# One hybrid decoder layer on eight cores: three phases in a row, or projections and output layer placed between attention tasks

## The chip, the cores and the metric

The kernel runs on all eight cores of one Trainium2 chip, two cores for each of the four batch entries. The metric is the device time of the slowest core in microseconds (us). Six runs of the kernel before had a median of 803.76 us. Some runs of any kernel on all cores fall into a slower state of the chip (one of these six did, with 835.79 us). Engines: PE is the matmul array, PEld its weight loads, DVE the vector engine, ACT the activation engine, POOL the GpSimd engine, SP the engine that issues plain transfers.

## The reference

```python
z = h @ w_in                                  # (B, 4096, 3072): q, k, v, gate, u, pool gate
s = einsum('bqhcd,bkhcd->bhcqk', q, k) / 8    # 4 heads, two halves c of width 64
a = softmax(where(causal, s, -inf))           # per half
o = (a[:, :, 0] - lam * a[:, :, 1]) @ v       # differential attention
o = rms_norm(o, subln_g) * (1 - lam_init) * silu(g_attn)
y = (trailing_mean_over(2, 4, 8, 16)(u) - u) @ w_pool * scale * silu(g_pool)
h = layer_norm(ALPHA * x + concat(o, y) @ w_out, ln_g, ln_b)
h = h + (p @ w_pe) * sigmoid(h @ w_pg + b_pg)
```

Width is 1024, sequence 4096, four heads. Each core makes keys and values for the whole sequence of its batch entry, and everything else for its half of the queries.

## The kernel before

The program has an in-order list of work for each engine, and a helper adds the semaphore waits from what each operation reads and writes. It runs in three phases. First come all projections, over eight accumulator banks in turn:

```python
for kc in range(8):                                   # one chunk: 8 matmuls of 512 columns
    matmul(ps[:, bank, :], win[:, kc, fc*128:(fc+1)*128], xbuf[:, kc, :], ...)
evac_copy(bank, kT[:, h, s*GT:(s+1)*GT], ...)         # DVE and ACT in turn
```

Then comes attention, one key block of 128 against 512 queries at a time:

```python
matmul(ps[:, 2*sl+c, q0:512], kT[64*c:64*c+64, h, keys], qT[64*c:64*c+64, h, queries])   # QK, c = 0, 1
activation(PT[pi], ps[:, 2*sl:2*sl+2], Exp)                                              # ACT, 1,024 wide
tensor_tensor(Lacc, Lacc, PT[pi], add)                # DVE: row sums; every second or third step
                                                      # goes to PE instead, as ones_bf @ PT
matmul(ps[:, 4+c, q0:512], Vt[keys, head], PT[pi][:, c, q0:512])                         # AV, V stationary
...
```

At the end comes the output layer, one tile of 128 tokens after another: `w_out`, layer norm, transpose, `w_pg`, sigmoid, `w_pe`.

The softmax here doesn't subtract the row's maximum and nothing guards it: scores larger than these inputs give would overflow.

## Time and profile before

| | before |
|---|---|
| median of six runs | 803.76 us |
| profiled run, slowest core | 805.6 us, mean granted clock 0.978 |
| busy: PE, DVE, ACT | 719.5, 562.3, 437.5 us |
| projections / attention / output layer | to 260 / to 643 / to the end |

A busy PE is not one at its peak, because matmuls overlap and their ends are modelled. The clock column is the share of full array clock that was granted.

### The profile page before, as it was taken

How to read it: one execution, taken by the hardware profiler on the slowest of the kernel's cores; microseconds unless marked ns; L12 is line 12 of the kernel's file. 1: busy time of each engine (PE TensorE's matmuls, PEld its weight loads, DVE VectorE, ACT ScalarE, POOL GpSimd, SP SyncE). 2: the span in 40 equal slices, each digit the busy share in tenths (PEclk: the TensorE clock that was granted, in tenths of full speed). 3: DMA queues.
4: the chain of work that ended last, by engine and by line, in shares of the span. 5: the costliest groups of instructions: out<-in, count | busy, mean ns of one | idle time of the engine just before them, and what ended most of it. 6: DMA issues, size and time to landing. Idle time of an engine off the chain costs nothing.

```text
span 805.6 us, 8871 instructions; the slowest of 8 cores (795.8 to 805.6 us)
## 1 busy us (share of the span) xinstructions
PE 719.5 (89%) x3496; PEld 278.6 (35%) x3496; DVE 562.3 (70%) x665; ACT 437.5 (54%) x526; POOL 87.3 (11%) x76
## 2 busy tenths in 40 slices
PE   0798999999999978888889889989898989999994
PEld 0343444444443322222222222222222335445441
DVE  0121723624535678888899989989889988888883
ACT  0012112112122889999989898999899932222221
POOL 6000000000000100000000000000000024544551
PEclk9999999999999999999999999999999999999997
DMA  8998330330300980000000000000003013343321
GB/s 89 141 158 112 53 52 1 53 53 0 53 1 0 137 152 0 1 1 1 0 1 1 0 1 1 0 1 1 1 0 131 1 52 105 106 147 115 105 105 52
DMA packets 28106, 39.96 MB, mean 50 GB/s; under 512 B 7328, under 2 KB 21024, under 8 KB 28064
## 3 DMA queue, kind: packets, MB, share of 16 engines
q0 software_dynamic: 22160, 20.81, 18.8%
q1 hardware_dynamic: 5904, 18.59, 7.3%
q8 instruction: 27, 0.44, 0.2%
q14 instruction: 15, 0.12, 0.0%
HBM read 51.81 MB, written 8.39 MB: 75 GB/s over the span
## 4 chain that ended last, share of the span: by engine, by line
PE 65%; DVE 14%; ACT 14%; DMA 3%; issue 2%; POOL 1%; another core or an unknown queue 0%; DVEq 0%; ACTq 0%; POOLq 0%
PE psum_all L332 20%; PE psum_all L545 9%; ACT sb_PT L520 8%; DVE sb_Lacc L531 7%; PE psum_all L372 7%; PE psum_all L727 6%; PE psum_all L667 6%; PE psum_all L505 6%; DMA sb_win<-w_in 3%; PE psum_all L550 3%; PE psum_all L714 2%; ACT sb_PT L516 2%; ACT sb_rr L571 2%; PE psum_all L702 2%; ACT sb_rr L575 1%
## 5 line engine op out<-in xcount | busy, mean ns | idle before, releaser
L531 DVE TENSOR_TENSOR sb_Lacc<-sb_Lacc,sb_PT 128x1024 f32<-128x1024 f32 (+1 forms) x200 | 232.0, 1160 | 28.3 <-ACT sb_PT L520 18.0
L520 ACT ACTIVATE sb_PT<-psum_all 128x1024 bf16<-128x1024 f32 (+3 forms) x256 | 228.9, 949 | 27.7 <-PE psum_all L505 16.4
L332 PE MATMUL psum_all<-sb_xb,sb_win 128*128 128x512 bf16 x768 | 170.2, 384 | 20.8 <-DMA sb_win<-w_in 20.8
L545 PE MATMUL psum_all<-sb_PT,sb_Vt 128*128 128x512 bf16 (+3 forms) x640 | 185.7, 373 | 0.6
L505 PE MATMUL psum_all<-sb_qT,sb_kT 64*128 64x512 bf16 (+3 forms) x640 | 120.9, 375 | 22.2 <-ACT sb_PT L520 18.3
L332 PEld LDWEIGHTS psum_all<-sb_xb,sb_win 128*128 128x128 bf16 x768 | 75.6, 99 | 113.3 <-issue 25.0
L505 PEld LDWEIGHTS psum_all<-sb_qT,sb_kT 64*128 64x128 bf16 x640 | 30.6, 93 | 159.8 <-ACT sb_PT L520 90.3
L516 ACT ACTIVATE sb_PT<-psum_all,sb_maskb 128x1024 bf16<-128x1024 f32 x64 | 67.8, 1110 | 6.0 <-PE psum_all L505 3.6
L686 POOL TENSOR_SCALAR sb_mv<-sb_mv 128x1 f32<-128x1 f32 x16 | 21.0, 1311 | 399.6 <-DVE sb_mv L679 399.6
L372 PE MATMUL psum_all<-sb_win,sb_xb 128*128 128x512 bf16 x256 | 58.3, 387 | 4.2 <-DMA sb_win<-w_in 4.2
L545 PEld LDWEIGHTS psum_all<-sb_PT,sb_Vt 128*128 128x128 bf16 x640 | 40.5, 98 | 59.9 <-issue 53.9
L667 PE MATMUL psum_all<-sb_wout,sb_mixT 128*128 128x512 bf16 x256 | 57.9, 379 | 0.5 <-DVE sb_Vt L672 0.5
L550 PE MATMUL psum_all<-sb_PT,sb_ones_bf 128*128 128x512 bf16 (+2 forms) x208 | 58.1, 362 | 0.0
L727 PE MATMUL psum_all<-sb_wpg,sb_kT 128*128 128x512 bf16 x256 | 57.9, 379 | 0.0
L737 ACT ACTIVATE sb_Vt<-sb_Vt 128x1024 f32<-128x1024 f32 x16 | 16.9, 1057 | 73.8 <-DVE sb_Vt L733 73.8
L744 POOL TENSOR_TENSOR sb_qT<-sb_qT,sb_Vt 128x1024 f32<-128x1024 f32 x15 | 35.4, 2359 | 59.5 <-DVE sb_qT L740 59.5
L318 DVE CAST sb_Vt<-psum_all 128x512 bf16<-128x512 f32 x16 | 11.1, 692 | 43.2 <-PE psum_all L372 43.2
L323 ACT ACTIVATE sb_Vt<-psum_all 128x512 bf16<-128x512 f32 x16 | 9.6, 597 | 55.3 <-PE psum_all L372 55.3
L318 DVE CAST sb_kT<-psum_all 128x512 bf16<-128x512 f32 x16 | 11.1, 691 | 40.1 <-PE psum_all L332 40.1
L396 ACT ACTIVATE sb_gps<-psum_all 128x512 f32<-128x512 f32 x16 | 9.6, 597 | 52.3 <-PE psum_all L332 52.3
L372 PEld LDWEIGHTS psum_all<-sb_win,sb_xb 128*128 128x128 bf16 x256 | 25.4, 100 | 35.9 <-DMA sb_win<-w_in 4.7
L708 ACT ACTIVATE sb_kT<-psum_all 128x512 bf16<-128x512 f32 x32 | 17.4, 595 | 34.1 <-PE psum_all L702 34.1
(96 smaller groups left out, 664.8 us busy)
## 6 DMA issues: line engine op xcount, KB each, us to landing
sb_xb<-xT POOLq DMA_DIRECT2D x8, 1024.0 KB, 10.2
sb_kT<-x_own SPq DMA_DIRECT2D x16, 512.0 KB, 4.9
out<-sb_qT SPq DMA_DIRECT2D x16, 512.0 KB, 3.6
sb_win<-w_in POOLq DMA_DIRECT2D x5, 1024.0 KB, 46.3
sb_wout<-w_out POOLq DMA_DIRECT2D x1, 2048.0 KB, 18.4
sb_wpg<-w_pg POOLq DMA_DIRECT2D x1, 2048.0 KB, 31.1
sb_win<-w_in POOLq DMA_DIRECT2D x4, 256.0 KB, 19.9
sb_pTb<-pT POOLq DMA_DIRECT2D x1, 1024.0 KB, 34.7
```

Source lines behind the costliest of these rows:

```text
L318: P.op(DVE, lambda e: e.tensor_copy(out=out_ap, in_=src), reads=[B_bank[bank]], writes=wbufs)
L332: P.op(PE, lambda e, kc=kc: e.matmul(ps[:, bank, :], win[:, kc, fc * 128:(fc + 1) * 128], xbuf[:, kc, :], start=(kc == 0), stop=(kc == 7)) ...
L372: st_=(kc == 0), sp_=(kc == 7): e.matmul(o, a, b, start=st_, stop=sp_),
L505: P.op(PE, lambda e, c=c: e.matmul(ps[:, 2 * sl + c, q0:512], kT[64 * c:64 * c + 64, h, key0:key0 + 128], qT[64 * c:64 * c + 64, h, j * GT ...
L516: P.op(ACT, lambda e: e.activation(out=PT[pi][:, :, q0:512], in_=ps[:, 2 * sl:2 * sl + 2, q0:512], func=AF.Exp, bias=maskb[:, j:j + 1], sc ...
L520: P.op(ACT, lambda e: e.activation(out=PT[pi][:, :, q0:512], in_=ps[:, 2 * sl:2 * sl + 2, q0:512], func=AF.Exp), reads=[B_S[sl]], writes=[ ...
L531: P.op(DVE, lambda e: e.tensor_tensor(out=Lacc[lb][:, :, q0:512], in0=Lacc[lb][:, :, q0:512], in1=PT[pi][:, :, q0:512], op=ALU.add), reads ...
L545: P.op(PE, lambda e, c=c: e.matmul(ps[:, 4 + c, q0:512], Vt[:, s * 4 + kb, h * 128:(h + 1) * 128], PT[pi][:, c, q0:512], start=it["first"] ...
L550: P.op(PE, lambda e, c=c: e.matmul(ps[:, 6 + c, q0:512], ones_bf[:], PT[pi][:, c, q0:512], start=(it["li"] == (3 if j <= 1 else 5)), stop= ...
L667: P.op(PE, lambda e, nh=nh, kc=kc: e.matmul(ps[:, nh, :], mixT[:, kc, tsl(t)], wout[:, kc, nh * 512:(nh + 1) * 512], start=(kc == 0), stop ...
L727: P.op(PE, lambda e, nh=nh, kc=kc: e.matmul(ps[:, 4 + nh, :], hTb[:, kc * 128:(kc + 1) * 128], wpg[:, kc, nh * 512:(nh + 1) * 512], start= ...
L744: P.op(DVE if t == NTB - 1 else POOL, lambda e: e.tensor_tensor(out=ot[t % 2][:], in0=pg[:], in1=hh[t % 2][:], op=ALU.add), reads=[B_pg, B ...
```

## The change

The intent is to give the array work while attention waits for the exponentials. Attention is cut into 144 tasks in four stages, and between the parts of a task one chunk of the next group's projections, or in stage 3 of the output layer, is put as filler. Cores share queries out in blocks of 128. AV takes the probabilities as the stationary operand, and a column of ones in V gives the row sums for one more column per matmul. SiLU and sigmoid become tanh, and inputs are laid out for long transfers. The core of the diff, with cuts marked:

```diff
-P.op(DVE, ... tensor_tensor(out=Lacc[lb][:, :, q0:512], in0=Lacc[lb], in1=PT[pi], op=ALU.add))
-matmul(ps[:, 4 + c, q0:512], Vt[:, s*4+kb, h*128:(h+1)*128], PT[pi][:, c, q0:512], ...)
+mm(ps[:, bank, col:col+129], PT[:, pb, bi, c, off+b*128:off+(b+1)*128], Vt[:, kb, h, 0:129], ...)
 ...
+FB = 7                                    # the bank of every filler
+def slot_fill():
+    ...                                   # finishing steps of earlier heads that are due
+    if fill: fill.pop(0)(FB); return
+    acc[0] += ratio                       # ratio = chunks / slots of this stage, at most 1
+    if acc[0] >= 1.0: acc[0] -= 1.0; run_filler(FB)
+for k in range(n_by_stage[j]):
+    qk(i)                                 # scores into banks 0 to 3, then the exponentials
+    mask(prev)                            # DVE, diagonal blocks only
+    slot_fill()
+    av(prev)                              # into banks 4, 5, 6
+    if last task of the head: after_av(prev)   # fin0 now, fin1, fin2, fin3 in later slots
+    slot_fill()
+# chunks left over at the end of a stage run densely over banks 7, 0, 1, 2, 3
 ...
+def c_gp(g, p):                           # a filler: pool gate
+    proj_T(...); act(gps, ps, Tanh); stt(gps, gps, 1.0, ps[bank], add, mult)   # DVE frees the bank
+    pool_chain(g, p)                      # and 2 to 7 DVE operations at once
 ...
```

## The prediction

> **What bounds the kernel now.** I read the page's slices first, then the table of windows, the groups by line, the timeline for single costs. The slices are 20.1 us each:
>
> ```profile
> PE   0798999999999978888889889989898989999994
> DVE  0121723624535678888899989989889988888883
> ACT  0012112112122889999989898999899932222221
> PEclk9999999999999999999999999999999999999997
> ```
>
> Three phases in a row: projections to about 260 us, where ACT and DVE read 1 to 6 tenths; attention to about 650, where ACT and DVE read 8 and 9; the output layer to the end, where ACT reads 2. The windows (busy us of each engine, then the granted clock) say the same:
>
> ```profile
> 60.00:265.00 205.00, 199.39 (x940) 89.24 (x938) 89.66 (x155) 44.40 (x70) 7.93 (x9) 0.99 0.27 38
> 400.00:500.00 100.00, 89.77 (x449) 26.28 (x449) 93.54 (x96) 91.86 (x104) 0.00 (x0) 0.98 0.00 1
> 700.00:795.00 95.00, 92.43 (x465) 46.03 (x463) 77.48 (x82) 22.93 (x33) 44.74 (x31) 0.98 0.35 110
> ```
>
> The columns are PE, PEld, DVE, ACT, POOL, clock, DMA share, GB/s. PE is busy in all three, but in the middle one that is not work at full rate: 449 matmuls per 100 us are 223 ns each although nearly half are QK matmuls that run two at a time. The groups:
>
> ```profile
> L531 DVE TENSOR_TENSOR sb_Lacc<-sb_Lacc,sb_PT 128x1024 f32<-128x1024 f32 (+1 forms) x200 | 232.0, 1160 | 28.3 <-ACT sb_PT L520 18.0
> L520 ACT ACTIVATE sb_PT<-psum_all 128x1024 bf16<-128x1024 f32 (+3 forms) x256 | 228.9, 949 | 27.7 <-PE psum_all L505 16.4
> L516 ACT ACTIVATE sb_PT<-psum_all,sb_maskb 128x1024 bf16<-128x1024 f32 x64 | 67.8, 1110 | 6.0 <-PE psum_all L505 3.6
> ```
>
> So DVE (row sums of the softmax) and ACT (the exponentials) bound attention. Its array work, with the cadences below: QK 65 us, AV 127, row-sum matmuls 40, triangle masks and finishing 33, together 265 us in some 390. About 125 us of array time are lost there, while projections (1,024 matmuls of 512 columns) and output layer (576) stand outside and leave ACT idle.
>
> **Costs of single things.** From the timeline:
>
> ```profile
> 260.27 0.61 PE L505 MATMUL psum_all<-sb_qT,sb_kT 64*128 64x512 bf16 x4 [0.79 <-DVE sb_Vt L318]
> ...
> 278.77 0.28 PE L511 MATMUL psum_all<-sb_tri,sb_ident 128*128 128x128 bf16 x2
> 278.84 0.15 PEld L545 LDWEIGHTS psum_all<-sb_PT,sb_Vt 128*128 128x128 bf16 x2
> 278.89 0.49 PE L545 MATMUL psum_all<-sb_PT,sb_Vt 128*128 128x384 bf16 x2
> ...
> 284.64 0.39 PE L505 MATMUL psum_all<-sb_qT,sb_kT 64*128 64x512 bf16 x2
> 284.96 0.11 PEld L545 LDWEIGHTS psum_all<-sb_PT,sb_Vt 128*128 128x128 bf16 x2 [0.23 <-issue]
> 284.96 0.60 PE L545 MATMUL psum_all<-sb_PT,sb_Vt 128*128 128x512 bf16 x2
> ```
>
> Two 128-column matmuls with own weight loads take 278.77 to 278.89, 60 ns each. One QK pair lasts 0.39 us, two pairs 0.61: 0.22 us per pair of 512. From a QK pair to the next full-height matmul pass 0.32 us, 0.10 more than 0.22: the price of a switch. A projection chunk of 32 matmuls takes 6.91 us in the chain of waits, 216 ns each. The 32 halo matmuls of 64 columns start between 73.7 and 74.6 us, some 30 ns each, so a weight load per matmul is not itself a limit at 60 ns.
>
> **What the Trainium skill says.** "TensorE: Matmul & The Clock Gate", section Back-to-back issue gap, gives 56 ns isolated and about 81 ns sustained for 128 columns with a load each; the trace's 60 ns lies near the first, over short runs only. The same page, Part 1, has a limiter to 13/16 of the clock once three cores of a die run dense matmuls; here the dense projection phase of eight cores was granted 0.99, so this run does not show it, though one of six timed runs took 835.79 us. "ScalarE: Activation LUTs", section Table sets, puts exp and tanh into one set; the kernel before pays four table loads of 1,283 ns, the changed one, using exp, tanh and copies, should pay one. "VectorE: DVE Perf Modes", section The perf-mode tier table, gives two-tensor operations in bf16 double rate; the kernel before has none, so the new mask multiplies (256 elements) are an estimate of 0.29 to 0.42 us.
>
> **The change, part by part.** It is a rewrite with four ideas.
>
> (1) Query blocks of 128 instead of 512 are shared out between the two cores of a batch. Per head a core computes 34,816 score columns per half (8 times 0+1+2+3 blocks of 512, plus 4 times 2,560 on the diagonal) instead of 37,888: 8% fewer.
>
> (2) AV is turned round: the probabilities are the stationary operand and V with a column of ones moves, 129 columns. That removes the Lacc additions (232 us of DVE), the 208 row-sum matmuls (58 us busy), Lh/Ll and the Ln/Exp reciprocals. It adds weight loads: 2,176 AV matmuls at 60 ns, 131 us, against 127 before. Finishing now goes on partitions of queries: 3 to 6 us of DVE per head, 20 times, plus transposes.
>
> (3) Projections of the next group, and the output layer of the first 12 of 16 tiles, are placed between attention tasks as filler. Nothing of the array work falls away by this, it takes the slack.
>
> (4) Inputs are laid out contiguously; the first K projection starts on quarters; sigmoid and SiLU become tanh.
>
> Array work per stage, counted from the built instruction list (144 tasks: 12, 28, 44, 60; each one switch of 0.10 us; a chunk of 8 matmuls is 1.73 us):
>
> - Head: 20 chunks, 34.6 us.
> - Stage 0: 44 chunks 76.0; halo and pooling 3.6; QK 4.4; AV 160 x 0.06 = 9.6; switches and transposes 2.2. Sum 96.
> - Stage 1: 32 chunks 55.3; halo and pooling 1.9; QK 11.4; AV 416 x 0.06 = 25.0; rest 3.8. Sum 97.
> - Stage 2: the same filler 57.2; QK 18.5; AV 672 x 0.06 = 40.3; rest 5.4. Sum 121.
> - Stage 3: 12 tiles x 36 x 0.216 = 93.3; transposes 7.7; QK 25.5; AV 928 x 0.06 = 55.7; switches 6. Sum 188.
> - Tail: 4 tiles, 33 us.
>
> Together 570 us. ACT: 244 exponentials of 1,024 at 1.03, 24 at 0.81, 20 at 0.60, evacuations and tanh about 0.6 each, hT and h copies 32 at 1.05: some 410 us, of it 162 in stage 3 and 106 in stage 2. DVE: some 385, of it 145 in stage 3. So the array is the longest in every stage, but in stages 2 and 3 ACT follows closely.
>
> Waits on the path, my estimates: Head: 5 MB in bf16 (x and K, V, the other x, Q) must come in at the 141 to 158 GB/s of slices 1 and 2, so chunks wait for loads and attention starts near 52, 17 lost. Stage 0: x is loaded again only after its last reader, and the next chunk needs it: 10 (an x load took 10.2 from issue to landing); 6 more where AV of the next head waits until DVE has read the accumulators. Stage 1: 8 of that kind. Stage 2: tasks without filler need 2.05 of ACT against 1.33 of PE, some 12 tasks, 10 us, and 4 more. Stage 3: the copy of h sits in ACT's order ahead of its DVE work, and tanh waits for a DVE add: 20. Tail: DVE needs 8.6 per tile, plus the last chain and store: 15.
>
> Sum: 52 + 112 + 105 + 135 + 208 + 48 = 660 us.
>
> **The rivals.**
>
> Rival A, the load-matmul cadence is 81 ns and not 60: 2,176 x 21 ns = 46 us more, 705. For it: runs of 16 such matmuls never occur before. Against: the 30 ns of the halo run.
>
> Rival B, in-order coupling. PE, ACT and DVE each run strictly in order, so one wrong neighbour stalls all three; in stage 3 two engines are above 75% busy. If the engines reach there only the 68% that the array reached in the old attention (265 of 390), stage 3 takes 276 and the total is 730.
>
> Rival C, the interleaving is better than I allow: buffers and evacuations hide my waits after the head. Then 570 + 17 + 15 + some 10, about 612.
>
> Rival D, the clock. Denser array work on all cores brings the 13/16 grant in the ordinary runs too. On 520 us of array-bound time that is 23% more, +120, 780. Against: 0.99 over 205 us of dense work.
>
> Rival E: the loads in the head are not faster or the filler is hidden anyway, no gain. The 125 us of slack speak against; even A and B together stay under 787.
>
> **Range and chances.** Centre 660. C gives the lower side, A and part of B the upper: 612 to 712. Only D with B reaches the old time. Faster by over 2%: 0.97; within: 0.02; slower: 0.01.
>
> **What would show it.** Right: attention starts near 52; the slices of PE at 9 throughout and ACT at 5 to 9 from there to 610; one table load; AV matmuls in runs of 16 starting about 60 ns apart; PE bound in the chain of waits, with stage 3 around 208 long; DVE total near 385, ACT near 410. Wrong: AV starts 80 ns apart (A); PE idle ended by ACT or DVE of over 60 us in stage 3 (B); PE idle under 15 us after the head (C); a granted clock near 0.81 in a fast run (D). A time above 710 means that in-order waits were undervalued, one below 612 that they were invented.

## The result, and the profile after

The changed kernel takes 783.78 us (median of 8 runs, 782.24 to 784.3). Ratios here are the mean time of one kernel's fast runs over that of the kernel before in the same rounds, so not quite the ratio of the medians. This one is 0.9747 (95% interval 0.973 to 0.9764). That is 2.5% faster, and far outside the predicted 612 to 712.

The slices of the changed kernel, 19.5 us each:

```profile
PE   3698786599899888799997957888877898897783
DVE  0102566535143365303214484667634646667674
ACT  0135342122667453577776623666566675671131
PEclk9899888799899999999999987999998899999897
```

No engine is full any more. DVE, which read 8 and 9 in the old attention, reads 0 to 8. ACT does not exceed 7, and PE falls to 5 to 7 again and again. By stages (edges at the first QK of each stage; the last edge, 702.7, lies 2.3 us before the end of the last AV; the columns are those of the windows in the prediction):

```profile
0.00:59.70 59.70, 39.88 (x162) 16.38 (x162) 3.52 (x12) 10.93 (x18) 10.43 (x23) 0.94 0.96 150
59.70:198.00 138.30, 109.67 (x667) 52.59 (x666) 74.58 (x162) 43.27 (x65) 6.73 (x9) 0.89 0.15 27
198.00:319.40 121.40, 106.19 (x854) 55.04 (x854) 53.30 (x120) 68.22 (x88) 5.83 (x7) 0.96 0.10 19
319.40:476.80 157.40, 132.57 (x1174) 73.38 (x1175) 56.52 (x124) 98.24 (x120) 5.75 (x7) 0.95 0.20 48
476.80:702.70 225.90, 193.26 (x1874) 113.20 (x1874) 130.36 (x235) 144.59 (x169) 35.71 (x30) 0.95 0.19 59
702.70:780.90 78.20, 53.82 (x255) 23.63 (x254) 51.24 (x81) 18.17 (x24) 13.82 (x11) 0.88 0.21 74
```

Against the prediction's 52, 112, 105, 135, 208 and 48 every piece is longer, most of all the tail (by 30 us) and stage 0 (by 26). The tail is not the four tiles of the prediction: the timeline has 240 of the output layer's matmuls after the last AV, and at 44 a tile that is five and a half. The plan itself leaves the rest over: it spreads all chunks but five over the slots, and finishing steps take some of these. In stage 0, where slots are fewer than chunks, 257 of some 440 filler matmuls ran after the last AV. The single costs were right, though. A run of AV matmuls in the timeline:

```profile
400.90 1.08 PE L283 MATMUL psum_all<-sb_Vt,sb_PT 128*128 128x129 bf16 x16
...
401.82 1.89 PE L283 MATMUL psum_all<-sb_X,sb_W 128*128 128x512 bf16 x8
```

Sixteen AV matmuls, each with its own weight load, pass from 400.90 to 401.82, 57.5 ns each (predicted 60). What the array waited for, over the whole run (us, times, longest; the first line, 19.8 us for the loads of the head, is left out):

```profile
...
PE psum_all L283 <- DVE sb_PT L298: 18.5, 12, 4.7
PE psum_all L283 <- ACT sb_PT L288: 12.6, 27, 1.6
PE psum_all L618 <- DVE sb_mixh L298: 12.3, 5, 5.2
PE psum_all L283 <- DVE sb_gps L301: 10.7, 7, 3.0
PE psum_all L691 <- ACT sb_dbf L288: 7.8, 3, 3.1
...
```

Most of it ends with DVE, which is busy only 47% of the time: masks (`sb_PT`), the finishing of a head (`sb_mixh`), and drains of the filler bank (`sb_gps`, `sb_U`). The timeline of stage 0, with rows left out at the dots, shows how a DVE that is half idle makes the array wait:

```profile
119.12 0.60 ACT L288 ACTIVATE sb_gps<-psum_all 128x512 f32<-128x512 f32 x1 [1.99 <-PE psum_all L283]
...
120.97 0.69 DVE L599 TENSOR_REDUCE sb_ms<-sb_TT 128x4 f32<-128x512 f32 x1
...
121.77 0.69 DVE L301 SCALAR_TENSOR_TENSOR sb_gps<-sb_gps,psum_all 128x512 f32<-128x512 f32 x1
...
122.52 0.39 PE L283 MATMUL psum_all<-sb_dbf,sb_wpool 128*128 128x512 bf16 x1 [3.00 <-DVE sb_gps L301]
123.16 1.51 DVE L298 TENSOR_TENSOR sb_TAB<-sb_TAB 128x564 f32<-128x564 f32 x2
...
125.60 0.48 DVE L298 TENSOR_TENSOR sb_PT<-sb_PT,sb_masks 128x256 bf16<-128x256 bf16 x2
...
125.95 1.92 PE L283 MATMUL psum_all<-sb_Vt,sb_PT 128*128 128x129 bf16 x16 [3.04 <-DVE sb_PT L298]
```

The gate chunk lies in bank 7, and ACT has read it at 119.7. DVE's own reading, which frees the bank, stands behind the finishing of a head and comes at 121.77. The next filler waits 3.00 us for it. Then the pooling chain, which nobody needs yet, goes ahead of two mask multiplies of a third of a microsecond, and AV waits another 3.04 us. After the second wait 16 AV matmuls take 1.92 us instead of 1.08. The clock goes with it. The columns are again those of the windows, first over a stretch at the end of another such wait (3.17 us, from 80.55 to 83.72), then over these 16 matmuls:

```profile
82.80:89.50 6.70, 5.78 (x26) 3.22 (x27) 2.74 (x8) 0.60 (x1) 1.04 (x1) 0.50 0.01 2
125.95:128.00 2.05, 2.05 (x17) 1.86 (x18) 2.02 (x5) 0.00 (x0) 0.00 (x0) 0.50 0.00 0
```

The array was granted half its clock, for 6.8 us in most such stretches. In this trace each of the 13 waits of over 2.5 us after the head met such a stretch, at the latest 1.2 us after its end (the wait that ended at 122.52 was still followed by a matmul at full clock); six other stretches came without a wait of that length.

A part of the mask waits seems to have another cause. In stage 3:

```profile
616.98 3.18 DVE L298 TENSOR_TENSOR sb_PT<-sb_PT,sb_masks 128x256 bf16<-128x256 bf16 x4
617.14 2.34 POOL L722 TENSOR_TENSOR sb_X<-sb_X,sb_ga 128x1024 f32<-128x1024 f32 x1 [7.54 <-DVE sb_ga L301]
```

One of these four masks takes 2.33 us, and it ends 0.14 us after an addition on POOL. Three masks of the 128 started during such an addition; they took 1.95 to 2.34 us, the others 0.285 (median). The array waited 5.5 of its 18.5 us for those three. Two other DVE operations with two operands in SBUF met the same fate (2.13 and 2.56 us instead of 0.23 and 0.42), while nine with at most one operand there ran at their usual length. No run here moves these additions.

### The profile page after: what moved, and what is told of

It reads as the page before. It is cut to its first block, busy times and chain, and to the rows that moved or that the text cites. A ratio compares the mean times of both kernels' runs of the same rounds, so it can differ in the third digit from the quotient of the medians.

```text
span 780.9 us, 11586 instructions; the slowest of 8 cores (773.0 to 780.9 us)
## 1 busy us (share of the span) xinstructions
PE 635.4 (81%) x4976; PEld 334.2 (43%) x4976; DVE 369.5 (47%) x731; ACT 383.4 (49%) x483; POOL 78.3 (10%) x86
## 4 chain that ended last, share of the span: by engine, by line
PE 53%; DVE 24%; ACT 11%; issue 4%; DMA 4%; POOL 2%; DVEq 0%; POOLq 0%
PE psum_all L283 53%; ACT sb_PT L288 6%; DVE sb_TT L298 5%; DMA sb_W<-w_in 3%; DVE sb_X L301 3%; DVE sb_TAB L298 2%; DVE sb_U L301 2%; DVE sb_PT L298 1%; ACT sb_gps L288 1%; ACT sb_W L288 1%; DVE sb_gps L301 1%; DVE sb_ga L301 1%; DMA sb_X<-xT 1%; DVE sb_ms L599 1%; ACT sb_dbf L288 1%
## 5 line engine op out<-in xcount | busy, mean ns | idle before, releaser
L288 ACT ACTIVATE sb_PT<-psum_all 128x1024 bf16<-128x1024 f32 (+2 forms) x288 | 263.8, 978 | 70.9 <-PE psum_all L283 70.6
L283 PE MATMUL psum_all<-sb_X,sb_W 128*128 128x512 bf16 x640 | 158.6, 398 | 28.1 <-DMA sb_W<-w_in 15.9
L283 PE MATMUL psum_all<-sb_Vt,sb_PT 128*128 128x129 bf16 x2176 | 156.7, 227 | 24.1 <-DVE sb_PT L298 18.5
L283 PEld LDWEIGHTS psum_all<-sb_Vt,sb_PT 128*128 128x128 bf16 x2176 | 136.7, 101 | 65.7 <-DVE sb_PT L298 23.6
L283 PEld LDWEIGHTS psum_all<-sb_X,sb_W 128*128 128x128 bf16 x640 | 61.5, 101 | 107.2 <-issue 32.2
L283 PE MATMUL psum_all<-sb_mixT,sb_kT 64*128 64x256 bf16 (+3 forms) x864 | 92.9, 311 | 15.6 <-ACT sb_PT L288 12.6
L283 PE MATMUL psum_all<-sb_W,sb_X 128*128 128x512 bf16 x384 | 95.5, 398 | 12.3 <-DMA sb_W<-w_in 4.0
L283 PE MATMUL psum_all<-sb_W 128*128 128x512 bf16 x320 | 84.2, 406 | 16.3 <-DVE sb_gps L298 4.4
L298 DVE TENSOR_TENSOR sb_PT<-sb_PT,sb_masks 128x256 bf16<-128x256 bf16 x128 | 39.3, 332 | 79.5 <-ACT sb_PT L288 78.0
L283 PE MATMUL psum_all<-sb_W,sb_mixT 128*128 128x512 bf16 x256 | 61.9, 390 | 6.6 <-ACT sb_W L288 3.2
L288 ACT ACTIVATE sb_Vt<-psum_all 128x512 bf16<-128x512 f32 x31 | 18.5, 597 | 53.9 <-PE psum_all L283 53.7
L288 ACT ACTIVATE sb_mixT<-psum_all 128x512 bf16<-128x512 f32 (+2 forms) x36 | 19.8, 549 | 46.8 <-PE psum_all L618 25.5
```

What stands on the lines that cost most here:

```text
L283: P.op(PE, lambda e: e.matmul(out, lhsT, rhs, start=start, stop=stop, skip_group_check=skip), reads=reads, writes=writes, sig=sig, deps=de ...
L288: P.op(ACT, lambda e: e.activation(out=out, in_=in_, func=func, scale=scale, bias=bias), reads=reads, writes=writes, deps=deps, cost=cact( ...
L298: dve(lambda e: e.tensor_tensor(out=out, in0=a, in1=b, op=op), reads, writes, n, deps, x)
```

## The experiments

Each edit is to the changed kernel, which stands at 783.78 us and ratio 0.9747; the combinations say what they start from. Theory A: filling stalls the array, because all fillers share one bank and because drains, masks and finishing share DVE's strict order. Theory B (narrower than the prediction's rival B): the coupling goes through ACT's order. Theory C: filling works, and the loss is between scores and exponentials. A fourth theory, that the half-rate clock makes the loss, was tested in the tail.

### No filling in stages 0 to 2 (noweave02), and none at all (noweave_all)

```diff
-ratio = min(1.0, (nch - 5) / nslots)
+ratio = 0.0 if j < 3 else min(1.0, (nch - 5) / nslots)     # noweave_all: 0.0 always
+dense(rest0[:4], ALLB)                                      # gates of group 0, needed at once
```

> Edit: in stages 0 to 2 no projection chunk is put between attention tasks; they all run afterwards, densely over five banks (the four gate chunks of group 0 run first). Theory A (the interleaving itself stalls the array: all fillers share accumulator bank 7, and their drains, the masks and the finishing queue in one strict DVE order): attention falls to the ACT bound, 161 us of exponentials in these stages, some 175 with finishing, the chunks run at 1.73 us, some 200, plus x loads; stages 0 to 2 take 375 to 400 instead of 417 and the time is 745 to 770. Theory C (the interleaving does gain what it was meant to, and the loss is in the coupling of scores and exponentials): the slack is given back, stages 0 to 2 take 440 or more, time over 800.

> Edit: as the run without interleaving in stages 0 to 2, and in stage 3 as well: the output layer of all 16 tiles runs after attention. Theory A: stage 3 and tail take 130 for attention (119 of exponentials) plus 16 tiles at 9.5 us as in the kernel before, 282 instead of 304, so about 725 to 750 in all. Theory C: interleaving the output layer gains in stage 3, 20 us or more slower than the run with only stages 0 to 2 changed.

Measured: 796.05 us (ratio 0.9885, 0.9843 to 0.9927) and 806.08 us (1.0004, 0.995 to 1.0057), both correct. Both predictions of A were too low: filling is worth 22 us in all (806.08 less 783.78), so it does gain, and not the 20 us or more that C asked for in stage 3 alone (10 us, 806.08 less 796.05). The run without any filling shows the pieces one by one. Its windows for attention in stages 0 to 3 and for the output layer (the edge at 607.7 lies 3 us before the end of the last AV):

```profile
67.70:106.00 38.30, 23.13 (x238) 16.39 (x238) 26.65 (x74) 21.50 (x28) 3.06 (x3) 0.82 0.00 1
192.20:258.00 65.80, 48.87 (x558) 31.33 (x558) 27.96 (x75) 51.41 (x59) 3.04 (x3) 0.95 0.01 1
318.50:413.60 95.10, 76.52 (x864) 48.44 (x864) 25.69 (x67) 80.75 (x90) 3.04 (x3) 0.95 0.00 1
488.80:607.70 118.90, 101.75 (x1388) 68.11 (x1390) 33.52 (x105) 110.78 (x125) 5.94 (x9) 0.97 0.14 33
607.70:802.30 194.60, 145.93 (x742) 66.37 (x739) 139.02 (x210) 54.00 (x68) 42.53 (x31) 0.93 0.23 79
```

Attention alone takes 318 us (38.3 + 65.8 + 95.1 + 118.9), where the old one took 383 (260.3 to 643.4). In stage 3 ACT is busy for 111 of 119: there it is at the bound of the exponentials. The array work in these 318 us is 210 (QK, AV, switches and transposes, from the prediction's sums), so 108 us of slack were there to be filled, and filling took 22. By stages (against this run's attention and chunks) it lost 6 us in head and stage 0, and gained 5, 13 and 9 in stage 1, in stage 2, and in stage 3 with the tail. The output layer takes 194.6 us, 12.2 per tile, though the array work of a tile is 8.3 and the kernel before, once under way, starts one every 8.6. In this run the transposes of a tile waited about 2 us for h (28.7 us in 13 waits). Its list of chunks puts them before the next tile's output projection, where the kernel before has them after it. The chain that ended last goes from the transposes over that projection, its layer norm and h to the copy of h and the next transposes, 10.4 us, and 12.1 where half clock met the projection. The run also shows that the rest of the rewrite gained nothing in all: it is level with the kernel before (1.0004), since attention is 65 us shorter, the output layer 32 and the projections 29 longer.

### A second filler bank in stage 3 (twobank3)

```diff
-run_filler(FB)
+run_filler([6, 7][n % 2])      # in stage 3 AV uses banks 4 and 5 only; n counts the fillers
```

> Edit: in stage 3, where bank 6 is not used by AV, fillers alternate between banks 6 and 7. Array idle time in stage 3 that was ended by a drain of bank 7 is some 13 us. Theory A with the single bank as its main part: 8 to 20 us faster than 783.8, and those waits gone. If the strict DVE order is what holds the drains and the bank only shows it: 0 to 4 us faster, the waits come back as waits on masks and finishing.

Measured: 775.47 us, ratio 0.9634 (0.9588 to 0.9681), correct: 8 us faster, the lower end of what the bank theory expected. In stage 3 the waits on drains are gone from the head of the list, and waits on exponentials have grown from 5.8 to

```profile
PE psum_all L283 <- ACT sb_PT L288: 18.2, 18, 4.5
```

The single bank was a true cause, and part of what it cost went over to the next wait.

### Drains by ACT alone (actdrain)

```diff
-tcopy(Uv, ps[bank])                                      # DVE
+act(Uv, ps[bank], AF.Copy)                               # ACT
-stt(gps, gps, 1.0, ps[bank], ALU.add, ALU.mult)          # DVE reads the bank (both gates)
+act(raw, ps[bank], AF.Copy); stt(gps, gps, 1.0, raw, ALU.add, ALU.mult)
```

> Edit: chunks of u and of both gates are emptied out of the bank by ACT alone (a copy in bf16 for the gates), so a bank no longer waits in DVE's order; DVE does the same multiplications from SBUF. Waits of the array ended by these DVE drains are 17 us in stages 0 to 2, with half-rate matmuls after the 3 us ones. Theory A, bank part: 12 to 25 us faster. If the DVE order binds elsewhere (masks, finishing): under 5 us faster, with more waits on masks and on the transposes' operand.

Measured: 779.99 us, ratio 0.9686 (0.9636 to 0.9736), correct: 4 us, under the 12 to 25 of the bank theory. The waits on `sb_gps` and `sb_U` left the top of the list, and the waits on masks rose from 18.5 us to

```profile
PE psum_all L283 <- DVE sb_PT L298: 27.9, 15, 6.4
```

That is close to what the alternative said: the bank was for the most part the messenger. Of the 9.4 us more, 7.1 lie while DVE was at other work (my sum over the timeline). The run is not clean, though: ACT got more to do as well (407.7 us busy, before 383.4), which can eat part of a gain.

### The pooling chain one operation per slot (spread)

```diff
-pool_chain(g, p)            # 2 to 7 DVE operations in one go
+lazy.append(each operation) # one taken per slot; the rest just before the pooling matmul
```

> Edit: the pooling chain's 3 to 7 DVE operations are not queued in one go at the gate chunk but one per slot, finished only before the pooling matmul needs them. Nothing is removed. Theory A, strict DVE order (masks, drains and finishing wait behind a burst of 2 to 4 us): waits of the array on masks (12 us in stages 0 to 2) and on finishing (12 us) shrink, 5 to 15 us faster. If order in DVE does not matter: within 3 us.

Measured: 771.65 us, ratio 0.9605 (0.9583 to 0.9627), correct: 12 us faster with the same operations in another order. This isolates DVE's order: nothing was removed, and 1.5% came from it. The waits fell where they were expected to, on masks from 18.5 us and on finishing from 12.3, together by 11.7:

```profile
PE psum_all L283 <- DVE sb_PT L298: 13.4, 11, 2.7
...
PE psum_all L634 <- DVE sb_mixh L298: 5.7, 4, 2.5
```

The drains of `sb_gps` did not change (10.7 us in both).

### Shorter tiles and two filler banks everywhere (split2), and put right (split1)

```diff
-tiles = [(0, 4)] if j < 3 else [(0, 2), (2, 4)]
+tiles = [(0, 2), (2, 4)]                       # split1: [(0, 4)] if j < 1 else ...
 # fillers alternate between banks 6 and 7     # split1: in stages 1 to 3
```

> Edit: attention works on two query blocks at a time in all stages, as stage 3 did, so bank 6 is free everywhere, and fillers alternate between banks 6 and 7 everywhere. The run with two banks in stage 3 alone gained about 8 us. Theory A, bank part: waits on drains of bank 7 in stages 0 to 2 are some 22 us; finishing of one head comes in two halves, so the bursts are shorter: 20 to 40 us faster than the changed kernel. If DVE order is the whole of it: about 8 to 12, what stage 3 alone gives.

> Edit: the run split2 put right: two query blocks at a time and filler banks 6 and 7 in stages 1 to 3 only, stage 0 as in the changed kernel (in stage 0 a head is so short that its finishing was overwritten by the next, which made that result wrong). Most of the gain of 21 us should stay, since stage 3 gave 8 and stages 1 and 2 have 121 and 157 us: 764 to 772, correct. If the wrong order in stage 0 was what gained: over 774.

Measured: split2 762.46 us, ratio 0.9474, with a wrong result (relative error 0.062): in stage 0 a head is one task long, and its finishing was overwritten by the next. Split1 is correct at 764.54 us, ratio 0.9514 (0.9485 to 0.9543), 19 us faster than the changed kernel. The edit has two parts, shorter finishing and the second bank; the second bank in stage 3 alone gave 8. How the other 11 divide was not measured.

### Keeping the clock up in the tail (warmtail)

```diff
+for _ in range(12): mm(ps[spare], wout[:, 0, 0:128], wout[:, 0, 0:512])    # unused results
 c_T(u)(nb())
```

> Edit: in the tail, twelve extra matmuls of 512 columns into a spare bank ahead of each tile's transposes, where the array waits up to 3.1 us for the copy of h; their results are not used. Theory of the clock (waits of about 3 us make the following matmuls run at half rate, which costs 6.7 us in the tail): 3 to 8 us faster than the changed kernel. If the half rate comes from something else, or costs nothing there: 0 to 4 us slower, since the extra matmuls take 2.6 us where the wait is shorter.

Measured: 785.32 us, ratio 0.9768 (0.9747 to 0.979), correct: nothing gained. The clock did rise, from the 0.88 shown for the tail above to 0.95, and the time that the tail's matmuls took beyond their normal cadence fell from 6.7 to 1.6 us (my sum over the timeline of each group's duration less its count times its cadence). But the run does not show that half rate costs nothing, because the extra matmuls cost about as much. The gate of one tile, first in the changed kernel, then here:

```profile
735.63 7.38 PE L283 MATMUL psum_all<-sb_W 128*128 128x512 bf16 x20 [1.12 <-ACT sb_W L288]
```

```profile
737.28 4.49 PE L283 MATMUL psum_all<-sb_W 128*128 128x512 bf16 x20 [1.12 <-ACT sb_W L288]
...
745.06 2.75 PE L283 MATMUL psum_all<-sb_W 128*128 128x512 bf16 x12
```

The higher clock saves 2.9 us, the extra twelve matmuls take 2.75, and from one tile's transposes to the next it is 12.1 us instead of 12.4. At the next tile the changed kernel was at full clock and did not wait for the copy of h, so the extra matmuls only cost: 12.2 us instead of 9.6. What half rate costs in the tail stays open.

### Two other orders in the output layer (tlate, hbdve)

```diff
-lst += [c_M(t, 0), c_M(t, 1)] ... c_T(t)                # transposes after the tile's own work
+lst += [c_M(t, 0), c_T(t - 1), c_M(t, 1)] ...           # tlate
-act(hb, y, AF.Copy)                                      # bf16 copy of h on ACT
+tcopy(hb, y)                                             # hbdve: on DVE
```

> Edit: a tile's transposes come after the first half of the next tile's output projection instead of before it, in stage 3 and in the tail. In the run without any interleaving every tile's transposes waited 2.05 us for the copy of h and a tile took 12.2 us. Theory (order of the output layer's chain costs the tail): those waits vanish in the tail's five tiles, 7 to 14 us faster with the half-rate matmuls after them. If the DVE's 8.6 us per tile is the limit already: under 4 us.

> Edit: the bf16 copy of h is made by DVE right after h instead of by ACT. ACT waited 16.7 us for h in stage 3 of the changed kernel and some more in the tail; with the copy on DVE its exponentials need not wait, and the tail's chain loses a change of engine and 0.4 us per tile. Theory B (coupling through ACT's order): 5 to 15 us faster. If ACT has slack there and DVE is the longer queue: 0 to 5 us slower, since DVE gets 16 times 0.69 us more.

Measured: tlate 788.75 us, ratio 0.9817 (0.9793 to 0.984); hbdve 789.78 us, ratio 0.9824 (0.9764 to 0.9883), both correct and both misses, 5 and 6 us slower. With the transposes late, stage 3 grew from 226 to 233 us, and the tail shrank from 78 to 76. With the copy on DVE, stage 3 grew to 233 as well. There ACT's waits for h are gone (32.4 us over the whole run of the changed kernel), but its waits for DVE's gate additions (`sb_gps`, `sb_ga`) grew from 53.4 to 91.1: the wait moved, because DVE is the longer queue. Theory B got no support. It isn't refuted, since the edit also gives DVE 11 us more work.

### Masks on POOL (maskpool)

```diff
-ttt(blk, blk, mk, ALU.mult, ...)                         # DVE
+P.op(POOL, tensor_tensor(out=blk, in0=blk, in1=mk, op=ALU.mult))
```

> Edit: the 128 mask multiplies go from DVE to POOL, which is 90% idle. Array waits that end with a mask are 18.5 us after the head. Theory A (the multiply of 0.33 us is late because other work stands ahead of it in DVE's order, not because it is long): 8 to 20 us faster although a multiply on POOL takes about twice as long. If the masks are late because the exponentials are late: no gain, or a few us slower by the longer multiply.

Measured: 794.51 us, ratio 0.9896 (0.9866 to 0.9925), correct: 11 to 12 us slower. POOL takes more than twice as long for a mask as DVE's 332 ns:

```profile
L558 POOL TENSOR_TENSOR sb_PT<-sb_PT,sb_masks 128x256 bf16<-128x256 bf16 x128 | 92.2, 731 | 179.8 <-ACT sb_PT L288 167.1 <-DMA sb_wpool<-w_pool 9.2
```

The array waited 21.5 us on masks instead of 18.5. The run doesn't tell a late mask from a slow one, so it is inconclusive on theory A. The timeline of the changed kernel tells more: of its 18.5 us of waits on masks, DVE was at other work for 9.1 and at masks for 8.7, the three that POOL held up included, and idle, with no exponentials to mask yet, for under 1 (my sum over the twelve waits). In the run spread the other work fell to 4.2 and the masks stayed at 8.7. So the masks are late by DVE's order and, as it seems, by POOL, hardly by late exponentials.

### Together (combo4, combo5, combo3, combo6)

Combo3 is spread, actdrain and split1 in one kernel. Combo6 adds the copy of h on DVE. Combo4 is combo3 with h issued directly after a tile's output projection, and combo5 adds the masks on POOL:

```diff
-[c_M(t, 0), c_M(t, 1)] ... c_G(t - 1, 0), ("h", t)
+[c_M(t, 0), c_M(t, 1), ("h", t)] ... c_G(t - 1, 0)       # combo4, combo5
```

> Edit: the pooling chain spread over slots, the drains by ACT, two blocks and two filler banks in stages 1 to 3, and in the output layer h of a tile issued directly after its output projection. Singly the first three gave 12, 4.5 and about 18 us. If they remove different waits: about 750. If all three shorten the same wait in DVE's order: 760 to 765. The early h should shorten the five tiles of the tail by 1 to 2 us each.

> Edit: as combo4, and the masks on POOL as well. Theory A: another 8 to 20 us faster than combo4, 730 to 745, the fastest of all; if the masks wait for exponentials: the same as combo4 or slower.

> Edit: the pooling chain spread over slots, drains by ACT, two query blocks and two filler banks in stages 1 to 3; h as in the changed kernel. Singly 12, 4.5 and 18 us faster than the changed kernel. If they remove different waits: 745 to 755, and correct. If they shorten the same wait: 760 to 765.

> Edit: combo3 with the copy of h on DVE. With the gain of hbdve on top of combo3, 735 to 748, the fastest of all; if ACT's wait is no cause, as combo3 within 3 us.

Measured: combo4 793.09 us (0.9873) and combo5 810.98 us (1.0101), both with a wrong result (relative error 0.13). The copy of h has one buffer, and with the early h it is overwritten before the tile before has been transposed. In combo4 ACT waited 85 us for h (55.0 and 30.2, against 32.4 in the changed kernel), and the exponentials stood behind it.

Combo3 is correct at 754.35 us, ratio 0.9379 (0.9336 to 0.9422), the fastest of all kernels here. The single gains of 12, 4 and 19 add up to 35, and it gained 29 (783.78 less 754.35): they remove mostly different waits. Combo6, 756.56 us (0.9411, 0.9368 to 0.9454), lies 2 us behind it. In combo3 the two longest waits of the array after the head are

```profile
PE psum_all L283 <- ACT sb_PT L288: 25.3, 36, 4.5
PE psum_all L283 <- DVE sb_PT L298: 22.9, 16, 3.2
```

on exponentials and on masks.

## Why the prediction was wrong

The direction was right, with 0.97 on faster, and so were the prices of single things: 57.5 ns per AV matmul against 60, 332 ns per mask against 290 to 420, DVE 369.5 us against 385, ACT 383.4 against 410, one table load. Rivals A (81 ns) and D (a granted clock near 0.81 throughout) did not come. Nor did C, and B's sign of over 60 us of idle array in stage 3 did not come either (32.6). Two readings were loose: the old attention ended at 643 and took 383 us, and DVE reads 7 in one slice of the projections.

The step that failed is the sum of "waits on the path", and behind it the sentence that filling "takes the slack". I took every stage as its array work plus 90 us of waits in all. In the table by stages the array is idle for 20, 29, 15, 25, 33 and 24 us, 145.5 in all, where I had 17, 16, 8, 14, 20 and 15; and it is busy for 635 us where I had 570, some 41 of that by half rate (below). The run without filling gives another bill. Its pieces one after another take 802.3 us on the slowest core. With all 108 us of attention's slack filled they would take 694. The changed kernel takes 784. So some 90 of the missing 124 us (784 less 660) is slack that was not filled, and some 34 are pieces that were longer than I had them.

**Slack.** Filling brought 22 us of 108. The cause that the runs show is the one that rival B named, engines that run strictly in order, but I looked for it in the wrong place: my sum had it with 20 us in stage 3, mostly on ACT, and the rival had it in stage 3 alone. It sat mostly in DVE, and in all stages. Spreading the pooling chain changed nothing but DVE's order and gave 12 us. The one bank for all fillers, plain in the diff as `FB = 7`, does not occur in my working at all; a second one gave 8 us in stage 3 alone. DVE's mean load hides this (47% measured): an engine that is half idle on average is late when what is urgent stands behind 3 us of what is not.

**Pieces.** Attention started at 59.7 us instead of 52. The output layer without filling needs 12.2 us per tile, where I had 8.3 of array work and, in the tail, 8.6 of DVE work. Its chain over transposes, output projection, layer norm, h and copy is longer than either. Reordering that chain twice in the changed kernel (tlate, hbdve) brought nothing; the order of the kernel before was not tried in the run without filling, so what would shorten it stays open. And the tail had five and a half tiles where I had four.

**Half rate.** I hadn't counted that long waits are followed by half the clock. The windows show it, and over the whole run matmuls took some 41 us beyond their cadence, against 17 in the kernel before (the same sum over the timeline). How much of that is time is not known: the run warmtail paid for the higher clock with its extra matmuls, and for stages 0 to 2 the cost was not measured apart from the waits.

**Open.** Combo3 recovers 29 of the 90 us. In it the array still waits 48 us on exponentials and masks. Whether more buffers for probabilities would help was not tried, nor was an order in which POOL's additions don't meet the masks.

## What to carry to other kernels

Before counting on filler work, run the pieces without overlap once: their sum, and the slack in it, are the frame of what overlap can bring, if each piece is in its own best order. Then look, for each filler, at which bank or buffer it holds and behind what in the other engines' order its release stands, because mean load says nothing about that. Long chains of small operations that nobody needs soon belong between urgent ones, one at a time.

## What the Trainium skill lacked or had wrong

- "TensorE: Matmul & The Clock Gate", Back-to-back issue gap: its 81 ns sustained for 128 columns with a load each was too slow; in runs of sixteen, matmuls of 129 columns took 57.5 ns each, near its isolated 56 ns.
- The same page, Part 1: its idle window of about 3.4 us before the clock halves is close. Here waits of 3.17 and 3.01 us were enough: the clock fell to 0.50 some 2 us into each and stayed there for 6.8 us.
- The same page, Part 1: its 13/16 limit once three cores of a die run dense matmuls did not come in the kernel before, whose eight cores ran dense projections from 100 to 260 us at 1.00. It did come in a fast run, spread: in its tail, from 724.6 to 750.6 us, cores 0 to 3 were granted 0.81, with the array busy for only 22 of 26 us.
- "ScalarE: Activation LUTs", Table sets: that exp and tanh share a set holds, one load in the run. Its 2.7 us for one load did not show: in the kernel before, two ACTIVATEs with a load of 1,283 ns between them lie 1.30 us apart (245.45 to 246.75).
- "VectorE: DVE Perf Modes", The perf-mode tier table: its double rate for bf16 is given for 2,048 elements. At 256 the bf16 two-tensor multiply took 285 ns on DVE (median; the mean of 332 includes the three that POOL held up), where fp32 ones of 256 took 416 to 425 ns, 1.5 times as long and not twice.
